# Grouped attention heads: maxima in pairs on the halves of the rows, keys two tiles at a time, sums and one row copy moved between engines

## The chip, the cores and the metric

The kernel runs on one core of a Trainium2 chip. The metric is device time in microseconds (us) of one execution. Engines: PE is TensorE (PEld its weight loads), DVE is VectorE, ACT is ScalarE, POOL is GpSimd, SP is SyncE, which issues DMAs here. Each engine runs its own instructions in the order written and waits on semaphores for the others.

## What is computed

One layer of a diffusion backbone over 256 context tokens and 2048 latent tokens: a mixing sublayer (differential attention, grouped-query attention and a Mamba-2 scan, side by side), an output projection, and a SwiGLU FFN. The change is in the grouped-query attention of the latent tokens: four query heads of width 64, two key heads, 2048 latent and 512 cached keys:

```
s = jnp.einsum('bqkgd,bskd->bkgqs', qb, k) * 64 ** -0.5
p = jax.nn.softmax(s, axis=-1)
o = jnp.einsum('bkgqs,bskd->bqkgd', p, v)
```

## The kernel before, in words

The work is cut into eight *units* of one key head j and 512 query tokens, both query heads of that key head (r = 0, 1) together. A unit needs two things in turn.

`maxima` (L945) finds, for each query row, the largest score over the 2560 keys. For each r and each block q of 128 queries TensorE multiplies the 128 stacked rows of the queries (64 rows of the value rounded to fp32r and 64 rows of the remainder, tile qa) with the keys (`gk[j][:, 0]`, which holds the same 64 rows twice), 512 keys at a time, into a bank of PSUM (tile gm, L959). VectorE reduces each bank to one column (gmx, L960). There are 40 such pieces, in two banks that alternate (tag "t"). Then the maxima are reduced to one negated value (nm, L962), eight transposes turn them into rows (gpt, L967), and VectorE copies each row to row 64 of tile qb (L968), so that the score matmul itself subtracts the maximum.

`weighted` (L971) walks over 20 tiles of 128 keys. For a tile: four score matmuls into one of two double banks (gs, L981 over 128 rows, L982 over 65), one exp on ScalarE (ge, L984), and, two tiles later, the product with the values into half the columns for each r (gpo, L990), and the addition of the exps to a running sum, on VectorE for eight of the 20 tiles, on GpSimd for twelve (L998, L1000). The first tile of each engine is only kept, so VectorE adds seven times and GpSimd eleven. Five exp tiles are in flight. A short tail (`unit_tail`, L1006) adds the two sums (L1009), turns the result (gpx), sums over keys by 16 small matmuls (gpl, L1020) and divides, during the next unit.

The order is written out by hand: `weighted` is a generator with two stops for each key tile, and the loop at L1339 to L1347 advances the maxima of the *next* unit by one piece at each stop, and at every second stop the tail, the context attention (`contexts`, in units 1 to 3) and the split of the output weights (`weights`, L1392, from unit 4 on: load w_out by 128 rows, ScalarE rounds it, VectorE subtracts, L1399). SP's DMAs alone are placed by the framework's scheduler in this part. Maxima of unit 0 run ahead, in the last steps of the differential heads, on 1024 keys at a time in the double banks (`wide`); unit 7 has none to run for a next one.

Buffers that matter: banks "t", two of 512 columns, also used by transposes; banks "s", two of 1024 columns; ge 5 tiles; wor 2 tiles.

Of the kernel before, what the change touches and what calls it, by code (L numbers as in the profile page):

```python
# [21 lines left out]
KEYS = LAT + PAST  # L22
NKT = KEYS // 128
# [13 lines left out]
def run(gen):  # L37
    for _ in gen:
        pass
# [802 lines left out]
def attention(tc, I, rx, op, ada_group, const, cst, ident, identr, stk_d, v_d, mix_d, rstd_from, row_bc):  # L842
    nc = tc.nc
    V, S, G, PE = nc.vector, nc.scalar, nc.gpsimd, nc.tensor
    i2 = cst[:, C_I2:C_I2 + 64]
    dscale, gscale = 32 ** -0.5, 64 ** -0.5

    with ExitStack() as ax:
        kv = ax.enter_context(tc.tile_pool(name="kv", bufs=2, reuse_waits="tile"))
        ps_s = ax.enter_context(tc.tile_pool(name="aps_s", bufs=2, space=PSUM, reuse_waits="tile"))  # L850
        ps_t = ax.enter_context(tc.tile_pool(name="aps_t", bufs=2, space=PSUM, reuse_waits="tile"))

        def load(out, src, q=nc.sync):

            q.dma_start(out=out.bitcast(F32), in_=src)
# [78 lines left out]
        gp, gk, gv, gqs, nms = {}, [], [], {}, []  # L934

        def group_queries(ui):
            j, u = units[ui]
            t0 = CTX + 512 * u
            qa, qb = [kv.tile([128, 2, 512], F32R, name=f"q{a}{ui}", tag="q") if ui % 2 else
                      gp[0].tile([128, 2, 512], F32R, name=f"q{a}{ui}", tag=f"q{a}") for a in "ab"]  # L940
            load(qa, stk_d[8 + 2 * j:10 + 2 * j, :, t0:t0 + 512].rearrange("r p t -> p r t"))
            load(qb[0:64], stk_d[8 + 2 * j:10 + 2 * j, 0:64, t0:t0 + 512].rearrange("r p t -> p r t"))
            gqs[ui] = qa, qb

        def maxima(ui, wide=False):  # L945
            j, u = units[ui]
            qa, qb = gqs[ui]
            nm = nms[ui % 2]
            mx = c1.tile([128, 8, 5], F32, name=f"gmx{ui}", tag="gmx", bufs=2)
            for r in range(2):  # L950
                for q in range(4):
                    ql = qa[:, r, 128 * q:128 * q + 128]
                    pieces = range(0, KEYS, 1024 if wide else 512)
                    for i, c in enumerate(pieces):
                        w = min(KEYS - c, pieces.step)
                        ps = (ps_s if wide else ps_t).tile([128, pieces.step], F32, name=f"gm{ui}_{r}{q}{c}",
                                                           tag="s" if wide else "t")
                        for e in range(0, w, 512):
                            PE.matmul(ps[:, e:e + 512], ql, gk[j][:, 0, c + e:c + e + 512], start=True, stop=True)  # L959
                        V.tensor_reduce(mx[:, 4 * r + q, i:i + 1], ps[:, 0:w], AX.X, ALU.max)  # L960
                        yield
            V.tensor_reduce(nm[:, :, 64], mx[:, :, 0:len(pieces)], AX.X, ALU.max, negate=True)  # L962
            yield
            for r in range(2):
                pt = ps_t.tile([128, 4, 128], F32R, name=f"gpt{ui}_{r}", tag="t")
                for q in range(4):
                    PE.transpose(pt[0:66, q], nm[:, 4 * r + q], identr)  # L967
                V.tensor_copy(qb[64:65, r], pt[64:65].rearrange("p q t -> p (q t)"))  # L968
                yield

        def weighted(ui, sp, ps_o, tails):  # L971
            j, u = units[ui]
            qa, qb = gqs.pop(ui)
            po = ps_o.tile([128, 512], F32, name=f"gpo{ui}", tag="o")
            acc, held, es = {}, {}, {}
            for kt in range(NKT + 2):
                if kt < NKT:
                    ks = slice(128 * kt, 128 * kt + 128)
                    ps = ps_s.tile([128, 1024], F32, name=f"gs{ui}_{kt}", tag="s").rearrange("p (r t) -> p r t", r=2)
                    for r in range(2):  # L980
                        PE.matmul(ps[:, r], gk[j][:, 0, ks], qa[:, r], start=True, stop=False)  # L981
                        PE.matmul(ps[:, r], gk[j][0:65, 1, ks], qb[0:65, r], start=False, stop=True)  # L982
                    e = es[kt] = sp.tile([128, 2, 512], F32, name=f"ge{ui}_{kt}", tag="ge", bufs=5)
                    S.activation(e, ps, AF.Exp, scale=gscale)  # L984
                yield
                if kt >= 2:
                    k = kt - 2
                    e = es.pop(k)
                    for r in range(2):
                        PE.matmul(po[64 * r:64 * r + 64, :], gv[j][:, k], e[:, r],  # L990
                                  start=(k == 0), stop=(k == NKT - 1))
                    eng, nm = (V, "v") if k % 5 in (1, 3) else (G, "g")
                    if nm not in acc:
                        if nm not in held:
                            held[nm] = e
                        else:
                            acc[nm] = sp.tile([128, 2, 512], F32, name=f"ga{nm}{ui}", tag=f"ga{nm}")
                            eng.tensor_tensor(acc[nm], held[nm], e, ALU.add)  # L998
                    else:
                        eng.tensor_tensor(acc[nm], acc[nm], e, ALU.add)  # L1000
# [128 lines left out]
        with ExitStack() as dx:  # L1129
            sp = dx.enter_context(tc.tile_pool(name="dsp", bufs=2, reuse_waits="tile"))  # L1130
            ps_o = dx.enter_context(tc.tile_pool(name="dps_o", bufs=1, space=PSUM, reuse_waits="tile"))
# [127 lines left out]
            side, tails = ada(), iter(())  # L1259
            pvs = []  # L1260
            for step in range(4 * n + 7):
# [15 lines left out]
                a, b, c, d, v = at(0), at(1), at(2), at(3), at(4)  # L1277
# [47 lines left out]
        gsp = ax.enter_context(tc.tile_pool(name="gsp", bufs=2, reuse_waits="tile"))  # L1325
        ps_o = ax.enter_context(tc.tile_pool(name="gps_o", bufs=1, space=PSUM, reuse_waits="tile"))
        cpool = ax.enter_context(ExitStack())
        csp = cpool.enter_context(tc.tile_pool(name="ctx", bufs=2, reuse_waits="tile"))
        ctx = contexts(csp, ps_o)
        tails = [normed(gsp, heads[3].o, heads[3].rl[:, :, 0], n, "l3", store_latents(3))]  # L1330
        for ui in range(len(units)):
            more = iter(())
            if ui + 1 < len(units):
                group_queries(ui + 1)
                more = maxima(ui + 1)
            if ui == 1:
                gv.append(group_values(1))
                gk.append(group_keys(1))
            for i, _ in enumerate(weighted(ui, gsp, ps_o, tails)):  # L1339
                next(more, None)  # L1340
                if i % 2:
                    if tails and next(tails[0], run) is run:
                        tails.pop(0)
                    if 1 <= ui < 4:
                        next(ctx, None)
                    if ui >= 4:
                        next(wo, None)  # L1347
# [37 lines left out]
class OutProj:  # L1385
# [6 lines left out]
    def weights(self, pool):  # L1392
        nc = self.tc.nc
        for k in range(8):
            raw = pool.tile([128, 1024], F32, name=f"wor{k}", tag="wor")
            nc.sync.dma_start(out=raw, in_=self.I["w_out"][128 * k:128 * k + 128, :])
            yield
# [749 lines left out]
```

## Time and profile before

| what | value |
|---|---|
| median of 3 runs | 3765.96 us (3758.62 to 3768.18) |
| profiled execution | 3772.03 us, span 3770.2 us |
| busy shares | PE 95%, DVE 66%, ACT 47%, POOL 48% |
| chain that ended last | PE 75%, DVE 9%, POOL 6% |
| granted TensorE clock, mean | 0.969 of full speed |

A busy share is the part of the span in which the engine ran an instruction. The chain is the work that ended last, followed back at each step to what released it. A row of the order of time gives start, duration, engine, line, operation, out<-in by tile names, shapes and count; consecutive instructions of a kind are merged. In brackets stands the idle time before, and what ended it. Matmul ends are modelled and overlap, so a matmul's price is read from start to start.

### The profile page before, as it was taken

The page shows a single profiled execution, that of the slowest core. Times are in us where ns is not written, and L with a number is a line of the kernel's source. Part 1 is how long each engine was busy: PE and PEld are TensorE (multiplying, and loading weights), DVE is VectorE, ACT ScalarE, POOL GpSimd, SP SyncE. Part 2 cuts the span into 40 slices and gives each one's busy share as a digit, 9 for nine tenths or more (in the row PEclk, how much of TensorE's full clock was granted, in tenths as well). Part 3 has the DMA queues.
Part 4 walks back from the last instruction along what each step waited for, and adds up shares of the span by engine and source line. Part 5 has one row for each costly group of instructions (what it writes and reads, how often), then busy time and mean ns, then how long its engine had stood idle before and what let it go on. Part 6 is the DMA issues. An engine that isn't in the chain of part 4 may idle for free.

```text
span 3770.2 us, 53905 instructions
## 1 busy us (share of the span) xinstructions
PE 3586.9 (95%) x20178; PEld 2884.0 (76%) x20178; DVE 2490.2 (66%) x4092; ACT 1787.6 (47%) x2890; POOL 1797.8 (48%) x1448
## 2 busy tenths in 40 slices
PE   6999899988999999999999989999999999999998
PEld 4888699984555555454458879999999999888886
DVE  3666766658889888767746776656556555465476
ACT  3555545546888885444334443334334333333232
POOL 3334356645788886445544567774233232011011
PEclk8999899998999999999999999999999999999999
DMA  5111244345311103001014656665454444645464
GB/s 199 49 46 46 76 126 124 119 130 164 97 34 42 36 22 83 14 26 48 23 62 165 209 190 216 213 216 182 153 186 164 160 154 163 231 160 175 153 217 156
DMA packets 265797, 473.65 MB, mean 126 GB/s; under 512 B 43480, under 2 KB 165752, under 8 KB 260928
## 3 DMA queue, kind: packets, MB, share of 16 engines
q1 hardware_dynamic: 247584, 456.72, 36.7%
q10 hardware_dynamic: 17232, 11.09, 1.1%
q8 instruction: 160, 2.62, 0.3%
q0 software_dynamic: 720, 2.38, 0.2%
q14 instruction: 101, 0.83, 0.1%
HBM read 345.72 MB, written 124.40 MB: 125 GB/s over the span
## 4 chain that ended last, share of the span: by engine, by line
PE 75%; DVE 9%; POOL 6%; issue 4%; DMA 3%; ACT 2%; SPq 0%; POOLq 0%; DVEq 0%; ACTq 0%
PE f L1685 6%; PE f L1684 6%; PE f L1683 6%; PE fy L1960 5%; PE fy L1962 5%; PE fy L1961 5%; PE ps L1174 4%; PE po L1234 4%; PE gpo L990 4%; PE px L225 3%; PE pt L1223 3%; PE gm L959 3%; PE gs L981 2%; PE gs L982 2%; PE opo L1447 2%
## 5 line engine op out<-in xcount | busy, mean ns | idle before, releaser
L1179 DVE TENSOR_SCALAR_CACHE_REDUCE e<-ps 128x1024 f32<-128x1024 f32 (+1 forms) x384 | 392.9, 1040 | 68.5 <-PE ps L1174 67.2
L1190 ACT ACTIVATE e<-e,nb 128x2560 f32<-128x2560 f32 x128 | 311.0, 2430 | 41.0 <-DVE nb L1184 40.9
L1960 PE MATMUL fy<-fp 128*128 128x512 f32 x792 | 308.7, 390 | 0.6 <-DVE fu L1823 0.6
L1962 PE MATMUL fy<-fp 128*128 128x512 f32 x792 | 308.7, 390 | 0.0
L1961 PE MATMUL fy<-fp 128*128 128x512 f32 x792 | 308.4, 389 | 0.0
L1212 POOL TENSOR_TENSOR e<-e,e 128x512 f32<-128x512 f32 x254 | 296.5, 1167 | 21.2
L1924 DVE TENSOR_TENSOR fp<-fo,fp 128x1536 fp32r<-128x1536 f32 (+1 forms) x110 | 208.7, 1911 | 140.5 <-ACT fp L1923 118.0
L960 DVE TENSOR_REDUCE gmx<-gm 128x1 f32<-128x512 f32 (+1 forms) x304 | 214.2, 715 | 120.0 <-PE gm L959 116.8
L1823 POOL TENSOR_TENSOR ft<-fu,fa 128x384 f32<-128x384 f32 x66 | 104.2, 1578 | 390.8 <-DVE fu L1823 342.8
L1991 POOL TENSOR_TENSOR fr<-fr,ln2b 128x1024 f32<-128x1024 f32 x17 | 54.0, 3178 | 490.6 <-DMA fo<-h_d 294.6
L1174 PE MATMUL ps<-dk,dq 96*128 96x512 f32 x640 | 244.9, 466 | 29.8 <-DVE e L1179 18.1
L1000 POOL TENSOR_TENSOR gag<-gag,ge 128x1024 f32<-128x1024 f32 x80 | 208.4, 2605 | 125.7 <-ACT ge L984 124.4
L984 ACT ACTIVATE ge<-gs 128x1024 f32<-128x1024 f32 x160 | 163.7, 1024 | 217.7 <-PE gs L982 215.3
L1923 ACT ACTIVATE fp<-fo 128x1536 fp32r<-128x1536 f32 (+1 forms) x110 | 157.2, 1442 | 195.1 <-PE fy L1962 163.8
L1211 POOL TENSOR_SCALAR e<-e,c 128x512 f32<-128x512 f32 x254 | 180.7, 711 | 115.2 <-DVE c L1203 104.9
L1174 PEld LDWEIGHTS ps<-dk,dq 96*128 96x128 f32 x640 | 101.0, 198 | 156.8 <-issue 72.1
L1224 ACT ACTIVATE wT<-pt 128x512 f32<-128x512 f32 x320 | 178.7, 591 | 67.8 <-PE pt L1223 67.1
L1234 PE MATMUL po<-wT,vl 128*64 128x256 f32 x1280 | 204.5, 407 | 0.0
L1223 PEld LDWEIGHTS pt<-cst,e 128*128 128x128 f32 x1280 | 160.7, 142 | 56.5 <-POOL e L1212 12.5
L1223 PE MATMUL pt<-cst,e 128*128 128x128 f32 x1280 | 197.1, 276 | 4.8 <-POOL e L1212 3.2
L225 PE MATMUL px<-xhTrue,wx 128*128 128x260 f32 (+2 forms) x864 | 182.1, 303 | 16.5 <-DVE l L374 7.0
L1685 PE MATMUL f<-fxt,wc 128*128 128x384 f32 x528 | 179.1, 339 | 2.6 <-DVE wc L1791 2.6
(454 smaller groups left out, 10613.0 us busy)
## 6 DMA issues: line engine op xcount, KB each, us to landing
fo<-in_wfo SPq DMA_DIRECT2D x110, 512.0 KB, 4.2
wq<-in_wfi SPq DMA_DIRECT2D x88, 512.0 KB, 3.7
wq<-ws_d SPq DMA_DIRECT2D x88, 512.0 KB, 4.2
h_d<-h SPq DMA_DIRECT2D x66, 384.0 KB, 3.0
wada<-in_w_ada SPq DMA_DIRECT2D x24, 1024.0 KB, 6.9
ws_d<-wq SPq DMA_DIRECT2D x44, 512.0 KB, 2.6
fo<-h_d SPq DMA_DIRECT2D x66, 256.0 KB, 4.1
fr<-x2T_d SPq DMA_DIRECT2D x20, 768.0 KB, 7.6
```

Source lines behind the costliest of these rows:

```text
L225: PE.matmul(out, l, r, start=(i == 0), stop=(i == n - 1))
L1174: PE.matmul(ps[:, 512 * c:512 * c + 512], Q[0:96, m, qs], K[0:96, m, k0:k0 + 512], start=True, stop=True)
L1179: V.tensor_scalar(self.e[m][:, k0:k0 + w], ps[:, c:c + w], dscale, -3.4e38, ALU.mult, ALU.max, accum_out=mx[:, m, seen[m]:seen[m] + 1])
L1190: S.activation(self.e[m], self.e[m], AF.Exp, bias=self.nb[:, m:m + 1], accum_out=self.l[:, m:m + 1])
L1212: G.tensor_tensor(e0[:, a:b], e0[:, a:b], e1[:, a:b], ALU.add)
L1223: PE.transpose(pt[:, k], self.e[0][:, 128 * (4 * g + k):128 * (4 * g + k) + 128], ident)
L1234: PE.matmul(po[64 * e:64 * e + 64], hd.v[:, k + e], self.wT[:, k + e], start=(k == 0), stop=(k == NKT - 2))
L1683: PE.matmul(o, w[:, 0, c, cs], x[:, 0, k], start=(k == 0), stop=False)
L1685: PE.matmul(o, w[:, 1, c, cs], x[:, 0, k], start=False, stop=(k == 3))
L1960: PE.matmul(o, x[:, 0, ts_], x[:, 0, hs], start=(f == 0), stop=False)
L1961: PE.matmul(o, x[:, 0, ts_], x[:, 1, hs], start=False, stop=False)
L1962: PE.matmul(o, x[:, 1, ts_], x[:, 0, hs], start=False, stop=(f == NF - 1))
```

## The change

- In `maxima` a piece is now a pair: for a block of queries and 512 keys, r = 0 on rows 0 to 63 and r = 1 on rows 64 to 127, of the rounded half of the queries alone (the remainder is left out of the maximum). Both read tile qb, whose lower half gets the rounded rows of r = 1 by a third load. Each matmul of a pair writes its own bank "t" (both in one double bank when wide). There are 20 stops of two matmuls instead of 40 of one; the wide form has 20 pieces instead of 24. The two transposed rows follow without a stop; the copy for r = 1 is on ScalarE.
- `weighted` takes two key tiles per round: eight score matmuls, a stop, then the value matmuls and additions of two tiles, a stop. The first round issues the matmuls that don't need the maxima first. VectorE gets five of the 20 tiles (k % 4 == 1), so four additions; GpSimd fifteen, so fourteen. Six exp tiles are in flight.
- The loop advances maxima, tail, context and weights once at each stop (21 stops a unit instead of 44).
- The output weights are loaded into one buffer, shared with a tile of another name, and used five stops later instead of two.

```
-            load qa, qb[0:64]
+            load qa, qb[0:64]; load(qb[64:128, 0], stk_d[9 + 2 * j, 0:64, t0:t0 + 512])
 maxima:
-            for r in range(2):
-                for q in range(4):
-                    for i, c in enumerate(pieces):
-                        PE.matmul(ps[:, e:e + 512], ql, gk[j][:, 0, c + e:c + e + 512], start=True, stop=True)
-                        V.tensor_reduce(mx[:, 4 * r + q, i:i + 1], ps[:, 0:w], AX.X, ALU.max)
-                        yield
+            for q in range(4):
+                for i in range(5):
+                    ...
+                    for r in range(2):
+                        hs = slice(64 * r, 64 * r + 64)
+                        PE.matmul(ps[r], qb[hs, 0, 128 * q:128 * q + 128], gk[j][hs, 0, 512 * i:512 * i + 512],
+                                  start=True, stop=True)
+                    if wide:
+                        V.tensor_reduce(mx[:, q::4, i], p, AX.X, ALU.max)
+                    else:
+                        for r in range(2):
+                            V.tensor_reduce(mx[:, 4 * r + q, i:i + 1], ps[r], AX.X, ALU.max)
+                    yield
 ...
-                V.tensor_copy(qb[64:65, r], pt[64:65].rearrange("p q t -> p (q t)"))
-                yield
+                if r: S.activation(qb[64:65, r], row, AF.Copy)
+                else: V.tensor_copy(qb[64:65, r], row)
 weighted:
+            def scores(kts):      # all first matmuls (128 rows), then per tile the second ones and the exp
+            def values(k):
+                ... value matmuls of tile k ...
+                eng, nm = (V, "v") if k % 4 == 1 else (G, "g")      # was k % 5 in (1, 3)
+            for kt in range(0, NKT + 2, 2):
+                if kt == 0:
+                    scores((0, 1))
+                elif kt < NKT:
+                    scores((kt,))
+                    scores((kt + 1,))
+                yield
+                if kt >= 2:
+                    values(kt - 2)
+                    values(kt - 1)
+                    yield
 loop:
-            for i, _ in enumerate(weighted(ui, gsp, ps_o, tails)):
+            for _ in weighted(ui, gsp, ps_o, tails):
                 next(more, None)
-                if i % 2: tail, ctx, wo
+                tail, ctx, wo
 weights:
-            raw = pool.tile([128, 1024], F32, name=f"wor{k}", tag="wor")
+            raw = pool.tile([128, 1024], F32, name=f"wor{k}", tag="osq", bufs=1)
             nc.sync.dma_start(out=raw, in_=self.I["w_out"][128 * k:128 * k + 128, :])
-            yield
+            for _ in range(4):
+                yield
```

## Rows read from the trace of the kernel before

**Rows 1.** Busy us of each engine (instructions) by unit, PEclk, DMA share, GB/s.

```profile
1535.60:1612.30 76.70, 69.94 (x294) 36.68 (x292) 56.20 (x105) 34.34 (x66) 30.73 (x14) 0.93 0.05 14
1612.30:1678.90 66.60, 66.60 (x295) 35.00 (x293) 41.36 (x77) 30.73 (x52) 32.52 (x16) 1.00 0.07 22
...
1736.20:1798.70 62.50, 57.90 (x231) 28.19 (x229) 53.04 (x61) 29.14 (x30) 30.61 (x12) 0.97 0.21 68
...
1854.90:1911.00 56.10, 55.42 (x231) 27.83 (x229) 39.09 (x53) 21.68 (x22) 29.65 (x12) 1.00 0.02 5
1911.00:1957.00 46.00, 44.90 (x182) 19.82 (x180) 14.10 (x12) 21.74 (x23) 27.41 (x12) 1.00 0.09 29
```

**Rows 2.** Chain that ended last, units 0 to 7: shares by line.

```profile
by line: PE gpo L990 28.2%; PE gm L959 18.0%; PE gs L981 14.9%; PE gs L982 14.6%; DVE gav L1000 4.1%; DVE gmx L960 3.9%; PE gpl L1020 2.5%; DVE wol L1399 2.0%; DVE gav L998 1.5%; issue 1.3%; PE poc L1107 1.0%; DVE qb L968 0.9%; PE pxc L1115
```

**Rows 3.** TensorE in time, unit 6: start, us, line, operation, shapes, count.

```profile
1897.41 0.50 PE L959 MATMUL gm<-gk,qa 128*128 128x512 f32 x1
1897.75 0.39 PE L981 MATMUL gs<-qa,gk 128*128 128x512 f32 x1
...
1898.67 0.40 PE L959 MATMUL gm<-gk,qa 128*128 128x512 f32 x1
1899.01 1.08 PE L990 MATMUL gpo<-ge,vg 128*64 128x512 f32 x4
1900.01 0.50 PE L959 MATMUL gm<-gk,qa 128*128 128x512 f32 x1
```

**Rows 4.** TensorE, unit 7, which has no maxima.

```profile
1946.48 0.50 PE L981 MATMUL gs<-qa,gk 128*128 128x512 f32 x1
...
1948.61 0.50 PE L981 MATMUL gs<-qa,gk 128*128 128x512 f32 x1
...
1954.00 2.79 PE L990 MATMUL gpo<-ge,vg 128*64 128x512 f32 x12
```

**Rows 5.** TensorE, context scores, 128 and 64 rows in turn (eight such).

```profile
1631.23 0.38 PE L1070 MATMUL psc<-ckq,cqa 128*128 128x256 f32 x1
1631.54 0.38 PE L1071 MATMUL psc<-ckq,cqa 64*128 64x256 f32 x1
```

**Rows 6.** TensorE, the scan's matmuls on the two halves of the rows.

```profile
316.69 0.70 PE L483 MATMUL po<-Sf,CT 64*128 64x256 f32 x4
317.32 0.39 PE L225 MATMUL px<-xhTrue,wx 128*128 128x260 f32 x1
```

**Rows 7.** VectorE in order of time, end of unit 6.

```profile
1904.92 1.25 DVE L1000 TENSOR_TENSOR gav<-gav,ge 128x1024 f32<-128x1024 f32 x1
...
1908.35 0.69 DVE L960 TENSOR_REDUCE gmx<-gm 128x1 f32<-128x512 f32 x1 [0.75 <-PE gm L959]
...
1909.19 2.15 DVE L1000 TENSOR_TENSOR gav<-gav,ge 128x1024 f32<-128x1024 f32 x1
```

**Rows 8.** GpSimd, the same stretch.

```profile
1902.70 2.38 POOL L1000 TENSOR_TENSOR gag<-gag,ge 128x1024 f32<-128x1024 f32 x1 [2.09 <-ACT ge L984]
1907.90 2.36 POOL L1000 TENSOR_TENSOR gag<-gag,ge 128x1024 f32<-128x1024 f32 x1 [2.82 <-ACT ge L984]
```

**Rows 9.** TensorE, from unit 6 to unit 7.

```profile
1907.81 0.50 PE L959 MATMUL gm<-gk,qa 128*128 128x512 f32 x1
...
1910.95 0.50 PE L981 MATMUL gs<-qa,gk 128*128 128x512 f32 x1
1912.12 0.50 PE L982 MATMUL gs<-qb,gk 65*128 65x512 f32 x1 [0.67 <-DVE qb L968]
```

**Rows 10.** VectorE groups, 1481 to 1960: busy us, mean ns | idle before.

```profile
L1000 DVE TENSOR_TENSOR gav<-gav,ge 128x1024 f32<-128x1024 f32 x48 | 72.8, 1516 | 22.2 <-ACT ge L984 22.2
...
L1399 DVE TENSOR_TENSOR wol<-wor,woh 128x1024 fp32r<-128x1024 f32 x8 | 14.6, 1824 | 0.0
```

**Rows 11.** Loads of the output weights (tile wor).

```profile
DMA to landing us min/median/max: 3.2/3.3/6.8
```

**Rows 12.** VectorE, the sum that closes unit 7.

```profile
1957.72 1.23 DVE L1009 TENSOR_TENSOR gav<-gav,gag 128x1024 f32<-128x1024 f32 x1 [3.18 <-POOL gag L1000]
```

More of the change, by code (lines that the diff above doesn't have):

```diff
@@ L942, in group_queries @@
             load(qb[0:64], stk_d[8 + 2 * j:10 + 2 * j, 0:64, t0:t0 + 512].rearrange("r p t -> p r t"))
+            load(qb[64:128, 0], stk_d[9 + 2 * j, 0:64, t0:t0 + 512])
             gqs[ui] = qa, qb
@@ L946, in maxima @@
             j, u = units[ui]
-            qa, qb = gqs[ui]
+            qb = gqs[ui][1]
             nm = nms[ui % 2]
             mx = c1.tile([128, 8, 5], F32, name=f"gmx{ui}", tag="gmx", bufs=2)
-            for r in range(2):
-                for q in range(4):
-                    ql = qa[:, r, 128 * q:128 * q + 128]
-                    pieces = range(0, KEYS, 1024 if wide else 512)
-                    for i, c in enumerate(pieces):
[L955 to L958, printed above, removed]
-                            PE.matmul(ps[:, e:e + 512], ql, gk[j][:, 0, c + e:c + e + 512], start=True, stop=True)
-                        V.tensor_reduce(mx[:, 4 * r + q, i:i + 1], ps[:, 0:w], AX.X, ALU.max)
-                        yield
-            V.tensor_reduce(nm[:, :, 64], mx[:, :, 0:len(pieces)], AX.X, ALU.max, negate=True)
+            for q in range(4):
+                for i in range(5):
+                    nm_ = f"gm{ui}_{q}{i}"
+                    if wide:
+                        p = ps_s.tile([128, 1024], F32, name=nm_, tag="s").rearrange("p (r t) -> p r t", r=2)
+                        ps = [p[:, r] for r in range(2)]
+                    else:
+                        ps = [ps_t.tile([128, 512], F32, name=f"{nm_}{r}", tag="t") for r in range(2)]
+                    for r in range(2):
+                        hs = slice(64 * r, 64 * r + 64)
+                        PE.matmul(ps[r], qb[hs, 0, 128 * q:128 * q + 128], gk[j][hs, 0, 512 * i:512 * i + 512],
+                                  start=True, stop=True)
+                    if wide:
+                        V.tensor_reduce(mx[:, q::4, i], p, AX.X, ALU.max)
+                    else:
+                        for r in range(2):
+                            V.tensor_reduce(mx[:, 4 * r + q, i:i + 1], ps[r], AX.X, ALU.max)
+                    yield
+            V.tensor_reduce(nm[:, :, 64], mx, AX.X, ALU.max, negate=True)
             yield
@@ L967, in maxima @@
                     PE.transpose(pt[0:66, q], nm[:, 4 * r + q], identr)
-                V.tensor_copy(qb[64:65, r], pt[64:65].rearrange("p q t -> p (q t)"))
-                yield
+                row = pt[64:65].rearrange("p q t -> p (q t)")
+                if r:
+                    S.activation(qb[64:65, r], row, AF.Copy)
+                else:
+                    V.tensor_copy(qb[64:65, r], row)
         def weighted(ui, sp, ps_o, tails):
@@ L975, in weighted @@
             acc, held, es = {}, {}, {}
[L976 to L979, printed above, removed]
+            def scores(kts):
+                ps = [ps_s.tile([128, 1024], F32, name=f"gs{ui}_{kt}", tag="s").rearrange("p (r t) -> p r t", r=2)
+                      for kt in kts]
+                for kt, p in zip(kts, ps):
@@ L980, in weighted @@
                     for r in range(2):
[L981 to L984, printed above, removed]
+                        PE.matmul(p[:, r], gk[j][:, 0, 128 * kt:128 * kt + 128], qa[:, r], start=True, stop=False)
@@ new lines, in scores @@
+                for kt, p in zip(kts, ps):
+                    for r in range(2):
+                        PE.matmul(p[:, r], gk[j][0:65, 1, 128 * kt:128 * kt + 128], qb[0:65, r],
+                                  start=False, stop=True)
+                    e = es[kt] = sp.tile([128, 2, 512], F32, name=f"ge{ui}_{kt}", tag="ge", bufs=6)
+                    S.activation(e, p, AF.Exp, scale=gscale)
+            def values(k):
+                e = es.pop(k)
+                for r in range(2):
+                    PE.matmul(po[64 * r:64 * r + 64, :], gv[j][:, k], e[:, r], start=(k == 0), stop=(k == NKT - 1))
+                eng, nm = (V, "v") if k % 4 == 1 else (G, "g")
+                if nm not in acc:
+                    if nm not in held:
+                        held[nm] = e
+                    else:
+                        acc[nm] = sp.tile([128, 2, 512], F32, name=f"ga{nm}{ui}", tag=f"ga{nm}")
+                        eng.tensor_tensor(acc[nm], held[nm], e, ALU.add)
+                else:
+                    eng.tensor_tensor(acc[nm], acc[nm], e, ALU.add)
@@ L985, in weighted @@
+            for kt in range(0, NKT + 2, 2):
[4 more added lines that the diff above has]
+                    scores((kt + 1,))
                 yield
                 if kt >= 2:
[L987 to L1000, printed above, removed]
@@ L1338, in attention @@
                 gk.append(group_keys(1))
-            for i, _ in enumerate(weighted(ui, gsp, ps_o, tails)):
+            for _ in weighted(ui, gsp, ps_o, tails):
                 next(more, None)
[L1341 to L1347, printed above, removed]
+                if tails and next(tails[0], run) is run:
+                    tails.pop(0)
+                if 1 <= ui < 4:
+                    next(ctx, None)
+                if ui >= 4:
+                    next(wo, None)
             run(more)
```

1 line of the change is left out of this document (removed).

## The prediction

> **What bounds the kernel now.** I read the page first, then the stretch of the grouped heads unit by unit, then its chain of waits, then single steps of TensorE, VectorE and GpSimd. The change touches only this stretch (about 1444 to 1957 us of 3770.2). It is eight units (0 to 7) of 20 key tiles. [rows 1] has five of them: units 1, 2, 4, 6 and 7. Unit 6 is a plain one: 56.1 us, TensorE busy 55.42 of them, VectorE 39.09, ScalarE 21.68, GpSimd 29.65. Units 1 and 2 also carry the context attention (76.7 and 66.6 us), unit 4 the split of the output weights (62.5), and unit 7 has no maxima for a next unit (46.0). The chain [rows 2] lies on the matmuls gpo, gm and gs for 28.2 + 18.0 + 14.9 + 14.6 = 76% of the stretch: TensorE sets the pace, and the maxima (gm) are the part of it that can shrink. VectorE has 17 us of slack in a plain unit, but only because its two banks for gm decouple it from TensorE.
>
> **The steady step on TensorE.** One key tile takes 2.60 us (gm at 1897.41 to gm at 1900.01) [rows 3]. The first matmul after a gpo takes 0.34 until the next, then each takes 0.23 (1897.75 to 1898.67 is four); the last one before gpo again 0.34; gpo 1.00. So two tiles cost 5.20. A tile more of gpo in the same run costs 0.85: twelve matmuls, three tiles, take 2.79 with entry and tail [rows 4].
>
> After the change two tiles are: eight gs, a pair, two gpo, a pair. Does a pair run side by side? No maxima do so now, but the scan's matmuls on the two halves of the rows do: four of 64 rows by 256 columns, fp32, are done in 0.63 (316.69 to 317.32) [rows 6]. One such fp32 pass of 512 columns on the full depth costs 0.43 (2.79 for six double steps) [rows 4], so of 256 it costs 0.21, four in a row 0.85, two side by side 0.43 plus entry and exit. I take it that the pair runs side by side. Its bare price is then 0.23. Each change of the array's shape costs more: matmuls of 128 and of 64 rows in turn, 256 columns each, follow at 0.31 [rows 5], where half of 0.23 would be 0.12; so 0.2 for a change, of which 0.1 falls before and 0.1 after it. The bounds for a pair with its changes are 0.23 (changes free) and 0.63 (two whole changes); I take 0.43, the value of [rows 5] with each change shared with its neighbour.
>
> The Trainium skill, "TensorEngine Tiling (Array Packing)", section Tiling Modes (Key Properties), says that a change of the tiling mode drains TensorE. That speaks against the change, as each pair stands between two other shapes; [rows 5] agrees with it. By that rule the pairs would eat their own gain wherever they stand between full-depth matmuls; here gpo, which uses half the columns, changes the shape anyway.
>
> New two-tile step: gs 0.34 + 7 x 0.233 + 0.1 = 2.07; pair 0.43; gpo 1.01 + 0.85 = 1.86; pair 0.43; sum 4.80 against 5.20. That is -0.2 a tile, -4.0 a unit, **-28.0** for the seven units with maxima. In unit 7 the step falls from 2.13 (1946.48 to 1948.61 [rows 4]) to (2.07 + 1.86) / 2 = 1.965: -3.4.
>
> **What takes it back: VectorE behind both banks.** Today a gm waits for the reduction before the last one. A pair takes both banks, so it waits for both reductions of the pair just before. Count from a pair's start: its first reduction starts 0.54 later (1907.81 on TensorE [rows 9], 1908.35 on VectorE [rows 7]), two take 1.4, so the banks are free at 1.95, and TensorE asks for them at 2.3 (over gpo) or 2.5 (over gs). That fits, with 0.35 to 0.55 to spare. Now put in an addition (one in two double steps, k = 5, 9, 13, 17). Queued behind it on VectorE are the next pair's reductions, and behind these TensorE. Alone it takes 1.25: it ends at 3.2, the next reductions at 4.6, the next pair but one is wanted at 4.8: no loss. But it waits for GpSimd: the add at 1909.19 took 2.15 and ended 1.08 after the GpSimd add of 1907.90 ended; the one at 1904.92, where GpSimd had 0.16 left, took 1.25 [rows 7, 8]. GpSimd gets 14 additions a unit for 11, three of 2.37 in a round of four tiles (9.6 us), so it runs 74% of the time, with 1.2 left on average when it does. Then the add holds VectorE for 2.4, to 4.4, the reductions end at 5.8, and the pair wanted at 4.8 starts its second half at 5.8: 1.0 lost. Bounds: 0 (GpSimd idle) and 2.2 (a whole GpSimd addition ahead). I take 1.0, four a unit, seven units: **+28.0**. Today's adds take 1516 ns on average [rows 10], 0.27 over the free one, with GpSimd busy 53% of unit 6 [rows 1] instead of 74%.
>
> The Trainium skill, "SBUF — State Buffer", section SBUF: two separate sides, calls this an exclusive lock that whoever starts first holds for the whole instruction. The two adds agree. By that rule the loss can't pass one GpSimd instruction for each add, which is my upper bound.
>
> **Unit ends.** The last two pairs follow each other with nothing between: the second is wanted after 0.43 and gets its banks at 2.0: +1.55. The row copies, one on ScalarE now, come while gpo of two tiles and the four first score matmuls run, so the present stall is gone: gs at 1912.12 came 1.17 after the one before instead of 0.34 [rows 9]: -0.85. The third tile of scores then waits for the first exp: +0.2. Net +0.9 x 7 = **+6.3**. The sixth exp buffer and one more load of 64 rows per unit cost nothing: by the steps above TensorE first reads the loaded tile some 9 us after the last scores release its place, and SP's queue holds nothing then but these loads and the unit's store; were it late, each microsecond would count for each unit.
>
> **The weight split** (8 times) now goes through one buffer, five steps apart (some 12 us), while such a load needs 3.3 (6.8 at most) [rows 11]: hidden; were SP held up, ScalarE and VectorE would wait for it in order. Its subtraction takes 1.82 on average with GpSimd's interference [rows 10], and costs 62.5 - 56.1 = 6.4 today, 0.8 each. With VectorE's slack down to some 0.35, 1.5 each: **+5.6**. Bounds -6.4 (hidden) and +8.2.
>
> **Context units.** They cost 76.7 + 66.6 - 2 x 56.1 = 31.1 over plain ones. Over unit 6 TensorE is busier by 14.5 + 11.2 = 25.7, VectorE by 17.1 + 2.3 = 19.4 [rows 1]: 45.1 in series, so 14.0 is covered today. Without the second bank I let half the cover go: **+7.0**, bounds 0 and +14.0.
>
> **Unit 7's end.** Its last two tiles are both GpSimd's now, and the sum that closes the unit waits for the later one, as it does today at 1957.72 [rows 12]. After the last exp that is one addition of 2.36 and the rest of another, some 1.4 more; with the -3.4: **-2.0**. The chain to the output projection starts there, so all of it counts.
>
> **Unit 0's maxima** (wide, before 1481): 40 x 0.233 + 24 x 0.1 = 11.7 becomes 20 x 0.53 = 10.7 (a pair between full-depth shapes): **-1.0**; the reductions keep their columns.
>
> Sum: -28.0 + 28.0 + 6.3 + 5.6 + 7.0 - 2.0 - 1.0 = +15.9. The profiled execution took 3772.0 (span 3770.2), 6 above the median of 3766.0, so I forecast 3766 + 16 = 3782, +0.4%. Its own range, with adds between 0.75 and 1.25 (+-7) and context between 3 and 11, is 3771 to 3793.
>
> **Rivals.**
> 1. *GpSimd is out of the way when the adds come* (faster). The adds cost nothing: +15.9 - 28.0 = -12, 3754. Place: the four adds of a unit; the point: GpSimd must have less than about 0.2 left when the first pair's reductions end. For it: the add at 1904.92 met just that [rows 7, 8]. Against: GpSimd is then 74% busy.
> 2. *Half of it* (no change). The adds cost 0.5, and the context units stay: +15.9 - 14.0 - 7.0 = -5, 3761. For it: adds and exps are both tied to TensorE's steps, so a round may settle at a good phase; against: the wait of [rows 7].
> 3. *The pair runs one after the other*, so that the change doesn't do what it says. TensorE then needs 140 x 0.23 = 33 more, part of it under VectorE's lateness; a third of it in view gives +11: 3793. Against it [rows 6]; for it: no pair of this type in the trace.
>
> **Chances.** The measurement can't tell less than 0.3% (11.3 us) from no change. Forecast 0.52, rival 1 0.18, rival 2 0.20, rival 3 0.10. Slower: 0.75 of the forecast and all of rival 3, 0.49. Same: the rest of the forecast and nine tenths of rival 2, 0.31. Faster: rival 1 and the rest of rival 2, 0.20. The range 3757 to 3797 leaves out most of rival 1 and the far ends of the unknown costs.
>
> **What would show it.** In the changed trace: two gm within 0.1 of each other (pair side by side; 0.23 apart: rival 3); steps of 4.8 for two tiles where no add falls, and about 1 longer where one does, with gav at 2 and more and the following gm waiting for gmx; unit 6 at about 57; units 1 and 2 together at 150; unit 7 at 44. A plain unit of 53 would prove rival 1, and wide waits of DVE for wor would break the weight term.

## The result, and the profile after

The changed kernel takes **3788.82 us** (median; 3777.45 to 3789.91), the kernel before 3764.02 on the same chip: ratio 1.0059 [1.0041, 1.0076], 24.8 us slower. The forecast was slower, by 15.9. The profiled execution after took 3789.13 (span 3787.3), 17.1 over that of before. The grouped heads account for +31.0 of these; the stretch ahead of them was 11.6 shorter and the one behind 2.2, in code that is the same. The 11.6 go with TensorE's granted clock: ahead of unit 0 the kernel before spent 174.1 us at half clock in this execution and the changed one 150.2, and half of the difference is 12. One execution of e4_before_no_pool below took 6804.28, and that kernel's median is over its other three.

Units again run from the first score matmul of one to that of the next. Unit 7 goes in these rows to just before the sum that closes it, as in [rows 1], and in the table further down to its last division. Busy time by engine for units 1, 2, 4, 5, 6 and 7, the view of [rows 1]:

```profile
1523.20:1612.70 89.50, 73.44 (x295) 37.65 (x294) 55.56 (x99) 34.43 (x68) 38.00 (x16) 0.83 0.05 14
1612.70:1686.30 73.60, 68.65 (x297) 35.02 (x294) 42.86 (x75) 30.62 (x54) 42.01 (x20) 0.93 0.07 20
...
1744.40:1811.10 66.70, 60.14 (x231) 28.60 (x229) 45.23 (x53) 25.15 (x28) 41.13 (x15) 0.88 0.16 49
1811.10:1875.90 64.80, 58.98 (x231) 28.29 (x229) 45.77 (x53) 25.08 (x27) 40.36 (x15) 0.90 0.14 44
1875.90:1931.70 55.80, 53.16 (x230) 26.66 (x229) 37.22 (x48) 21.05 (x23) 38.65 (x15) 0.99 0.02 6
1931.70:1976.00 44.30, 42.00 (x188) 21.95 (x185) 9.23 (x7) 22.12 (x25) 36.90 (x15) 1.00 0.10 30
```

The plain unit 6 did not grow (56.1 before); units 1 and 2 grew by 12.8 and 7.0, unit 4 by 4.2, and unit 5, plain before, by 8.6. Where a unit grew, the granted clock (third figure from the end) fell too: 0.83 and 0.93 in units 1 and 2, against 0.93 and 1.00, and 0.88 in unit 4, against 0.97.

TensorE in unit 6, the view of [rows 3]. A round has two pairs (`gm` x2): one follows the values (gpo), the other the scores (gs). From a pair that follows the values to the next such pair is a step of two tiles. The first row gives the first and the last start of the pair at 1890.65:

```profile
L963 PE MATMUL gm<-gk,qb x2: 500/500/500, 1890.7 to 1890.7; 64*128 64x512 f32 x2
1890.65 0.50 PE L963 MATMUL gm<-gk,qb 64*128 64x512 f32 x2
1891.08 0.74 PE L995 MATMUL gs<-qa,gk 128*128 128x512 f32 x2
...
1893.14 0.50 PE L963 MATMUL gm<-gk,qb 64*128 64x512 f32 x2
1893.58 1.94 PE L1006 MATMUL gpo<-ge,vg 128*64 128x512 f32 x8
1895.45 0.50 PE L963 MATMUL gm<-gk,qb 64*128 64x512 f32 x2
...
1897.94 0.98 PE L963 MATMUL gm<-gk,qb 64*128 64x512 f32 x2
...
1900.72 0.50 PE L963 MATMUL gm<-gk,qb 64*128 64x512 f32 x2
...
1905.51 0.50 PE L963 MATMUL gm<-gk,qb 64*128 64x512 f32 x2
...
1908.56 1.09 PE L963 MATMUL gm<-gk,qb 64*128 64x512 f32 x2 [0.48 <-DVE gmx L969]
...
1911.44 0.50 PE L963 MATMUL gm<-gk,qb 64*128 64x512 f32 x2
```

The two matmuls of a pair start together (less than 0.1 apart, the sign that the prediction asked for), take 0.50 together, and the next work starts 0.43 after the pair: they run side by side. A step without an addition takes 4.80 (1890.65 to 1895.45). Those with one take 5.27 (1895.45 to 1900.72) and 5.93 (1905.51 to 1911.44), and in each a pair comes late: the pairs at 1897.94 and 1908.56 take 0.98 and 1.09 instead of 0.50, the second matmul waiting for its bank, and the pair at 1908.56 waited 0.48 for the first bank as well. VectorE, then GpSimd, in the same stretch:

```profile
1894.88 2.29 DVE L1013 TENSOR_TENSOR gav<-ge,ge 128x1024 f32<-128x1024 f32 x1
1897.10 2.67 DVE L969 TENSOR_REDUCE gmx<-gm 128x1 f32<-128x512 f32 x4
...
1904.95 2.94 DVE L1015 TENSOR_TENSOR gav<-gav,ge 128x1024 f32<-128x1024 f32 x1
1907.83 2.56 DVE L969 TENSOR_REDUCE gmx<-gm 128x1 f32<-128x512 f32 x4
```
```profile
1893.72 18.84 POOL L1015 TENSOR_TENSOR gag<-gag,ge 128x1024 f32<-128x1024 f32 x7
```

GpSimd adds without a gap for 18.84 us, the two VectorE additions take 2.29 and 2.94 instead of 1.25, and four reductions then run without a gap: VectorE is behind by a pair, and TensorE waits for it. Groups of VectorE, units 0 to 6, the view of [rows 10]:

```profile
L1015 DVE TENSOR_TENSOR gav<-gav,ge 128x1024 f32<-128x1024 f32 x21 | 49.8, 2372 | 0.0
L1013 DVE TENSOR_TENSOR gav<-ge,ge 128x1024 f32<-128x1024 f32 x7 | 15.4, 2193 | 0.0
L1425 DVE TENSOR_TENSOR wol<-wor,woh 128x1024 fp32r<-128x1024 f32 x8 | 15.2, 1903 | 1.0 <-ACT woh L1424 1.0
```

The chain of waits of the changed execution does not lead back through the units, so nothing answers [rows 2]. TensorE's own waits in the grouped heads (us in total, times, longest) stand in for it; first before, then after:

```profile
PE gm L959 <- DVE gmx L960: 11.0, 11, 2.1
PE gs L982 <- DVE qb L968: 3.6, 6, 0.7
```
```profile
PE gm L963 <- DVE gmx L969: 27.1, 17, 6.1
PE ptc L1124 <- DVE gmx L969: 6.2, 8, 0.8
PE gs L995 <- ACT ge L1001: 5.0, 10, 1.2
PE pxc L1141 <- DVE gmx L969: 1.2, 6, 0.2
```

The wait for the row copies is gone, as forecast. New are the waits of ptc and pxc: these matmuls of the context attention use the same two banks "t" as the pairs. That GpSimd holds the exp tiles too long is hardly the cause: in the changed execution ScalarE's exps waited once for a GpSimd addition, for 1.2.

### The profile page after: what moved, and what is told of

It is laid out like the page before. It is cut to its first block, busy times and chain, and to the rows that moved or that the text cites. A ratio compares the mean times of both kernels' runs of the same rounds, so it can differ in the third digit from the quotient of the medians.

```text
span 3787.3 us, 53927 instructions
## 1 busy us (share of the span) xinstructions
PE 3577.3 (94%) x20178; PEld 2873.9 (76%) x20178; DVE 2469.7 (65%) x4056; ACT 1784.6 (47%) x2898; POOL 1872.8 (49%) x1472
## 5 line engine op out<-in xcount | busy, mean ns | idle before, releaser
L1205 DVE TENSOR_SCALAR_CACHE_REDUCE e<-ps 128x1024 f32<-128x1024 f32 (+1 forms) x384 | 392.7, 1039 | 67.4 <-PE ps L1200 66.4
L1216 ACT ACTIVATE e<-e,nb 128x2560 f32<-128x2560 f32 x128 | 311.0, 2430 | 41.0 <-DVE nb L1210 40.9
L1015 POOL TENSOR_TENSOR gag<-gag,ge 128x1024 f32<-128x1024 f32 x104 | 280.9, 2701 | 75.6 <-ACT ge L1001 69.4
L969 DVE TENSOR_REDUCE gmx<-gm 128x1 f32<-128x512 f32 x280 | 180.0, 684 | 142.5 <-PE gm L963 142.1
```

Source lines behind the costliest of these rows:

```text
L1205: V.tensor_scalar(self.e[m][:, k0:k0 + w], ps[:, c:c + w], dscale, -3.4e38, ALU.mult, ALU.max, accum_out=mx[:, m, seen[m]:seen[m] + 1])
L1216: S.activation(self.e[m], self.e[m], AF.Exp, bias=self.nb[:, m:m + 1], accum_out=self.l[:, m:m + 1])
```

## The experiments

The theory tested is the forecast's: VectorE's additions wait for GpSimd, and since a pair needs both banks, TensorE waits behind them. The rival is that another part of the change costs, GpSimd's three additions more or the order of two tiles. All kernels were timed beside the kernel before. The table has each kernel's profile by kind of unit (us, worked out from the starts of the units; "half" is the time at half clock in all eight). These columns come from one profiled execution each. "Change" is the median against that of before on the same chip:

| run | 0+3+6 plain | 1+2 context | 4+5 weights | 7 | half | change |
|---|---|---|---|---|---|---|
| before | 167.6 | 143.2 | 118.7 | 51.9 | 19.3 | |
| after | 169.3 | 163.1 | 131.4 | 50.4 | 84.4 | +24.8 |
| e1_split_before | 173.1 | 166.7 | 129.5 | 47.4 | 83.0 | +30.9 |
| e2_split_alone | 167.5 | 143.5 | 116.3 | 52.4 | 25.3 | -5.7 |
| e3_after_no_pool | 155.5 | 145.9 | 110.6 | 47.4 | 23.9 | -25.7 |
| e4_before_no_pool | 164.7 | 133.0 | 110.4 | 50.6 | 0.8 | -27.5 |
| e5_after_all_pool | 165.8 | 155.9 | 114.4 | 56.1 | 67.4 | +2.6 |
| e6_before_all_pool | 164.3 | 148.2 | 113.8 | 55.7 | 29.1 | -4.2 |
| e7_pairs_alone | 180.7 | 151.7 | 129.0 | 56.0 | 81.6 | +25.7 |
| e8_filler | 169.0 | 168.4 | 135.2 | 51.1 | 38.3 | +35.2 |
| e9_two_tiles_single | 159.0 | 147.1 | 128.4 | 50.8 | 34.3 | +3.9 |
| e10_two_tiles_single_split | 158.5 | 150.3 | 121.6 | 52.6 | 41.9 | -3.4 |
| e11_after_no_wol | 171.3 | 163.8 | 111.2 | 51.3 | 66.0 | +3.7 |
| e12_mixed | 160.2 | 145.3 | 123.9 | 52.8 | 37.2 | -4.9 |

**The split of the additions, in both kernels** (e1_split_before: the changed kernel; e2_split_alone: the kernel before).

```
e1:  - eng, nm = (V, "v") if k % 4 == 1 else (G, "g")
     + eng, nm = (V, "v") if k % 5 in (1, 3) else (G, "g")
e2:  the reverse
```

e1 

> The changed kernel with the additions divided as before (eight key tiles of 20 on VectorE, so seven additions, eleven on GpSimd). My theory (VectorE is late behind both banks, each addition of its own costs a wait for GpSimd and then a stall of TensorE): three more additions of 1.25 us a unit on VectorE outweigh the three fewer of 2.37 on GpSimd, as every one of them stands before a pair; plain units (0, 3, 6) about 1.5 us longer each than in the changed kernel, the whole 0 to +8 us against it, so +25 to +33 against the kernel before. Rival A (fourteen GpSimd additions are what is too much, whatever VectorE does): plain units shorter by 2 or more, the whole 15 to 25 us faster than the changed kernel, close to the kernel before. Rival B (neither; the cost is in the context and weight units alone): plain units unchanged, the whole within 4 us of the changed kernel.

e2 

> The kernel before with only the new division of the additions (four on VectorE, fourteen on GpSimd a unit); maxima singly, one tile at a time. My theory: with a bank between, VectorE's lateness is hidden, so the new division alone costs little: plain units 55.5 to 56.5, the whole within 6 us of the kernel before (context units up to 3 us longer each). Rival A (fourteen GpSimd additions are too much as such): +10 to +20 us.

Measured: 3793.72, ratio 1.0078 [1.0056, 1.0100]; and 3757.15, ratio 0.9986 [0.9977, 0.9996]. With GpSimd back at eleven additions the changed kernel is no faster (+30.9 against +24.8), and with fourteen the kernel before is no slower, but a little faster. The fourteen additions by themselves are not the fault.

**GpSimd's additions left out, in both kernels** (only the first of a unit stays, so the sums are not complete; the closing sum adds 1.0, which the lines below leave out). That is 13 additions a unit fewer in e3 and ten in e4.

```
-                else:
+                elif eng is V:
                     eng.tensor_tensor(acc[nm], acc[nm], e, ALU.add)
```

e3 

> The changed kernel without GpSimd's additions but the first of each unit; the closing sum adds 1.0 so that no divisor is zero, so the output is not the reference's. My theory (two of VectorE's waits for GpSimd make each addition cost 1 us of TensorE, the same in context and weight units): plain units 52 to 53.5 instead of 55 to 58, units 1, 2, 4, 5 down by 12, 7, 11, 9 us, the stretch 35 to 50 us shorter than in the changed kernel. Rival B (the context and weight units suffer from the coarser steps, not from GpSimd): plain units as theory, but units 1, 2, 4, 5 together no more than 10 us shorter.

e4 

> Control: the kernel before without GpSimd's additions but the first of each unit, with the same 1.0 in the closing sum (output not the reference's). My theory: with a bank between, GpSimd's additions cost the plain units next to nothing (55 to 56.1), and only units 1 and 4, where VectorE is nearly full, gain some 7 us each: 12 to 25 us less than the kernel before, so some 20 us less gain than the same step brings in the changed kernel. Rival A (GpSimd's additions cost the same in both): the gain equals that of the changed kernel within 5 us.

Measured: 3737.17, ratio 0.9927 [0.9911, 0.9943], so 50.5 under the changed kernel (24.8 + 25.7, each against before on its chip); and 3735.31, ratio 0.9931 [0.9905, 0.9956], 27.5 under before. GpSimd's additions cost some 23 us more in the changed kernel, which is nearly its whole loss; without them the two kernels can't be told apart. The eight units of e3 are 54.7 shorter than those of the changed kernel, a little more than expected. Units 1 and 6 of e3, then TensorE's waits in units 0 to 7:

```profile
1518.40:1595.20 76.80, 68.62 (x295) 35.09 (x293) 43.44 (x99) 34.19 (x68) 3.69 (x3) 0.91 0.05 16
...
1827.40:1879.80 52.40, 51.28 (x232) 25.72 (x229) 32.89 (x49) 21.09 (x23) 3.47 (x2) 1.00 0.02 6
```
```profile
PE ptc L1124 <- DVE gmx L969: 5.7, 8, 0.8
PE gm L963 <- DVE gmx L969: 4.9, 8, 0.8
PE gs L995 <- ACT ge L1001: 4.6, 10, 1.2
```

The same units of e4:

```profile
1525.00:1591.40 66.40, 64.75 (x294) 34.20 (x292) 49.02 (x104) 34.20 (x66) 4.72 (x4) 1.00 0.06 17
...
1824.20:1879.30 55.10, 55.09 (x230) 27.87 (x228) 37.63 (x53) 21.66 (x22) 3.46 (x2) 1.00 0.02 6
```

The wait of `gm` falls from 27.1 to 4.9 and unit 6 to 52.4. What stays is ptc, and scores that wait for exps (4.6, of which 2.8 in units 1 and 2). Unit 1 is 10.4 longer than its counterpart even here, and both context units 12.9, at a granted 0.91 in unit 1 against 1.00. TensorE waits there for the banks "t" that the pairs hold, without GpSimd's help (ptc and pxc, 6.9), and for the banks "s", which exps and the context's own scores give back late (4.3); these are no matter of the pairs' two banks.

**All additions on GpSimd, in both kernels** (no closing sum).

```
-  eng, nm = (V, "v") if k % 4 == 1 else (G, "g")      # e6: k % 5 in (1, 3)
+  eng, nm = G, "g"
-  V.tensor_tensor(acc["v"], acc["v"], acc["g"], ALU.add)
```

e5 

> The changed kernel with all twenty additions of a unit in one sum on GpSimd, none on VectorE, and so no closing sum. My theory (VectorE's additions wait for GpSimd while TensorE needs both of its banks): with no addition in VectorE's queue the wait is gone, although GpSimd has five additions more (19 x 2.37 = 45 us in a unit of some 53); 28 to 45 us shorter than the changed kernel's 3789, at 3744 to 3761, plain units at 52 to 53. Rival (GpSimd is simply the bound, or its load on the memory is the fault): with 19 additions it is worse, 3789 or longer, plain units at 57 or more.

e6 

> The kernel before with all additions on GpSimd in the same way. Theory: single maxima have a bank in hand, so VectorE's waits cost little there; 5 to 15 us shorter than before (the split by four alone gave 5.7). If the gain is that of the same edit in the changed kernel (28 or more), the pairs have nothing to do with it.

Measured: 3766.95, 22.2 under the changed kernel; 3760.12, 4.2 under before. Both fell short of the gains expected (28 to 45, 5 to 15). Five additions more on GpSimd make the changed kernel faster, so it is the additions' place in VectorE's queue that costs, not GpSimd's load. Two units of e5 are longer than in the changed kernel: unit 7 (56.1 against 50.4), where TensorE waits at the end for the last of GpSimd's additions, and unit 6 (59.9 against 55.9). The first row is that wait in unit 7; then TensorE in unit 6, with the busy time of the first 17.2 us of the unit:

```profile
PE gpl L1044 <- POOL gag L1015: 7.5, 1, 7.5
1846.28 0.68 PE L976 MATMUL gpt<-identr,nm 128*66 128x128 f32 x8 [1.99 <-DVE nm L971]
...
1856.01 2.79 PE L1006 MATMUL gpo<-ge,vg 128*64 128x512 f32 x8
...
1873.22 0.50 PE L963 MATMUL gm<-gk,qb 64*128 64x512 f32 x2
...
1878.02 0.50 PE L963 MATMUL gm<-gk,qb 64*128 64x512 f32 x2
```
```profile
1846.80:1864.00 17.20, 17.20 (x61) 10.64 (x58) 4.51 (x7) 6.20 (x7) 7.28 (x4) 0.62 0.00 1
```

The later step is 4.80 again, without a wait; unit 6 is long because TensorE, after a wait of 1.99, did its first 17.2 us at a granted 0.62.

**Pairs alone** (one tile at a time, one pair in each, additions as before).

```
before + the paired `maxima` and the load of qb[64:128, 0]
-                next(more, None)
+                if i % 2 == 0 or i > 40:
+                    next(more, None)
```

> The kernel before with the maxima in pairs alone: one tile of keys at a time, a pair in each, the additions split as before, both row copies on VectorE. Theory: a tile's step is 1.14 + 0.43 + 1.01 = 2.58 on TensorE, as before, and the pair takes both banks, so an addition that waits costs up to 0.6; with seven additions in seven units 0 to 29 us longer than before, I take +12, plain units 57 to 59. Rival (it is the order of two tiles that costs, the pairs alone are harmless or a gain): -5 to +2.

Measured: 3789.97, ratio 1.0058 [1.0044, 1.0071]: +25.7, inside the range but twice the value taken. The pairs alone bring a loss as large as the whole; the order of two tiles is not needed for it. The loss falls in other units, though: the plain ones grew by 13.1 (54.0, 65.0 and 61.7, where 57 to 59 was expected) against 1.7 in the changed kernel, the context units by 8.4 against 19.9. TensorE, then VectorE:

```profile
1889.41 0.50 PE L963 MATMUL gm<-gk,qb 64*128 64x512 f32 x2
...
1891.97 0.50 PE L963 MATMUL gm<-gk,qb 64*128 64x512 f32 x2
...
1894.87 1.10 PE L963 MATMUL gm<-gk,qb 64*128 64x512 f32 x2 [0.27 <-DVE gmx L969]
```
```profile
1891.15 3.07 DVE L1008 TENSOR_TENSOR gav<-ge,ge 128x1024 f32<-128x1024 f32 x1
```

A tile takes 2.56 where nothing waits, as before (2.60). Behind an addition of 3.07 the next pair waits 0.27 for its first bank and takes 1.10 instead of 0.50.

**Filler for TensorE** (the changed kernel, units 1, 2, 4 and 5).

```
+ for p in ps:
+     for r in range(2):
+         PE.matmul(p[:, r], gk[j][:, 0, 0:128], qa[:, r], start=True, stop=True)
```

> The changed kernel with two matmuls more ahead of the scores of each tile in units 1, 2, 4 and 5 (they write where the scores then start afresh, and are read by nobody): 160 matmuls of 0.23, 37 us of TensorE. Theory (TensorE's stalls lower its granted clock, and the half clock is some 17 us of the surplus): TensorE idles less, the time at half clock in these four units falls from 70 us to under 25, and the units get longer by less than half of the added work, or shorter: -15 to +15 us. Rival (the clock falls for another reason, and the surplus is all VectorE's waiting): half-clock time stays near 70, and the units get longer by 15 to 37.

Measured: 3799.55, 10.4 over the changed kernel. Units 1 and 5:

```profile
1523.90:1613.90 90.00, 75.70 (x335) 42.14 (x334) 55.12 (x99) 34.87 (x67) 36.61 (x16) 0.94 0.05 14
...
1815.50:1884.40 68.90, 64.36 (x271) 34.03 (x270) 41.54 (x53) 25.97 (x27) 39.62 (x15) 0.95 0.16 48
```

In the four units the time at half clock fell from 70.3 to 23.9, and 37 us of added work cost 9.1. So the clock rose when TensorE was given more to do, and the rival is out. The traces also say where the 28 saved come from. TensorE's busy time in the four units rose from 261.2 to 276.8, by 15.6 for 37 of added work, so the same work took some 21 less at the higher clock; its idle time fell from 33.4 to 26.8, by 7 that the filler merely fills.

**Two tiles without pairs** (e9: single maxima, four in the scores of two tiles, weights through one buffer as in the change; e10: also the new split and one row copy on ScalarE).

```
+ for r in range(2):
+     PE.matmul(ps[:, r], gk[j][:, 0, ks], qa[:, r], start=True, stop=False)
+     PE.matmul(ps[:, r], gk[j][0:65, 1, ks], qb[0:65, r], start=False, stop=True)
+     if r: ... exp
+     yield
+ ... after two tiles: values(kt - 2); values(kt - 1)
```

e9 

> The kernel before with the order of two tiles alone: eight score matmuls with one single full-depth maximum after every second of them, then four value matmuls in one run; additions split as before, weights through one buffer as in the change. Theory (the pairs that take both banks are the fault, the longer run of value matmuls is a gain): a step of two tiles is 12 x 0.233 + 0.34 + 0.1 + 1.6 = 4.85 on TensorE against 5.20, up to -3.5 a unit where VectorE follows; four maxima in some 3 us need 2.8 of VectorE, so additions cost part of it; -25 to -5 us on the whole, I take -12. Rival (the order of two tiles is at fault as well): 0 to +15.

e10 

> The kernel before with all of the change but the pairs: two tiles with single maxima as in the run beside it, four additions of a unit on VectorE (the split that alone gave -5.7), one row copy on ScalarE. Theory: the gains add up, -30 to -8 us against before, I take -17, which would beat both kernels. Rival: VectorE's additions wait longer behind a busier GpSimd and the split no longer gains; equal to the run beside it or longer.

Measured: 3768.16, ratio 1.0004 [0.9993, 1.0014]; 3760.94, ratio 0.9990 [0.9981, 0.9999]. Both missed. The plain units did gain (159.0 and 158.5 against 167.6), but the context and weight units gave it back (in e9 +3.9 and +9.7). There the waits of `gm` for VectorE came to 22.0 in e9, against 9.6 before: four maxima in a row within three microseconds leave VectorE little room, as pairs do. In the weight units no run splits this from the weights' one buffer.

**The changed kernel without the weights' subtraction.**

```
- nc.vector.tensor_tensor(self.wl[:, k], raw, self.wh[:, k], ALU.subtract)
+ nc.scalar.activation(self.wl[:, k], raw, AF.Copy)
```

> The changed kernel with the weights' subtraction left out (the low half of the output weights becomes a plain copy on ScalarE, so this part of the computation is changed). Theory: the subtraction waits for GpSimd as the additions do, and units 4 and 5 (66.7 and 64.7 us) fall to about 56 to 58 each, the whole by 10 to 18 us to 3771 to 3779. Rival (units 4 and 5 are long for the additions and the clock alone): they stay above 61, the whole falls by less than 7.

Measured: 3768.02, 21.1 under the changed kernel, a little more than expected. Units 4 and 5:

```profile
1744.00:1799.90 55.90, 53.21 (x231) 26.74 (x229) 37.33 (x49) 28.71 (x31) 38.67 (x15) 0.99 0.19 59
1799.90:1855.20 55.30, 52.64 (x232) 26.24 (x229) 37.36 (x49) 28.84 (x32) 38.59 (x15) 1.00 0.17 51
```

Eight subtractions cost the changed kernel 2.6 each, with the clock, which is lower where they stand (0.88 and 0.90 against 0.99 and 1.00).

**A mixed version** (e10, with the order of two tiles in units 0, 3, 6 and 7 only).

```
- for kt in range(NKT + 2):
+ for kt in range(NKT + 2 if ui in (1, 2, 4, 5) else 0):   # else two tiles, as in e10
```

> A version put together from the runs: single maxima everywhere, the order of two tiles only in units 0, 3, 6 and 7 (52.3, 53.1, 53.1, 52.4 in the run with that order and the new split), one tile at a time in units 1, 2, 4 and 5 (76.9, 66.6, 59.3, 57.0 in the run of the split alone), four additions on VectorE, one row copy on ScalarE, weights through one buffer. Theory (the longer run of value matmuls gains where VectorE has nothing else to do, and costs where it has): the units add up to 470.7 against 481.4 before, so 8 to 14 us shorter than before, about 3753, and 3 to 8 us shorter than the split alone. Rival (a unit is long or short by its phase against GpSimd and by the granted clock, not by its order): the sum comes back to about 480, no more than 5 us from before.

Measured: 3759.12, ratio 0.9993 [0.9983, 1.0002]: the rival was right. Units 0, 3, 6 and 7 kept their times within 2 us, but units 4 and 5 came to 123.9 instead of 116.3, with the weights through one buffer over two units. The lowest median of all versions that compute the whole result is that of the new split alone (3757.15, 5.7 under before), but this one and e6 (4.9 and 4.2 under) are too near to tell apart from it.

## Why the prediction was right in direction and short in size

**Right.** *The pair* runs side by side at 0.43 (forecast 0.43), so rival 3 is out. *The step* of two tiles is 4.80 to the hundredth. *What takes it back* is VectorE behind both banks: unit 6 shows it, and e3 and e5 (each against the same edit in the kernel before) and e7 support it from three sides. Without GpSimd's additions the plain units are 9.2 shorter than before's (e3 against e4), 3.1 each, and the forecast's -4.0 + 0.9 is -3.1. Rival 1 needed GpSimd out of the way, and the additions took 2.2 to 2.4 on average, as forecast. Rival 2 fell by its other half, context units that stay as they were; its price of an addition was the nearer one, as the next lines show. Two slips in the sum cancel: 20 x 0.53 is 10.6 and not 10.7, 20 x 0.165 is 3.3 and not 3.4.

**The added wait**, forecast at 1.0 per addition: three steps of unit 6 cost 0.47, 1.13 and 0.30 (the third 5.10, 1916.24 to 1921.34), so 0.63 on average, less than forecast. The *unit end* costs more: among other things the exps at a unit's start hold TensorE for 0.71 (before the scores of 1934.54) instead of 0.2. Together the plain units came to +0.6 each against +0.9, which is luck in part: by these three steps the additions would cost 2.5 a unit and not 4.0 (an estimate), and the unit ends made up for it. *Unit 7* came to -1.5 against -2.0, *unit 0's maxima* to -1.8 against -1.0. The loads through one buffer were hidden: VectorE waited 1.0 in all for the rounding that follows them.

**Too small: the context units.** Forecast +7.0 beside the plain +1.8, bounds 0 and +14.0; measured +19.9 in all, so 18.1 for this term. I had let half of the cover go. Without GpSimd's additions all of it is there already: these units are 12.9 longer (e3 against e4) where plain ones are 3.1 shorter each, 19.1 in all. The pairs hold both banks, and the context's transposes queue for the same two (ptc, 5.7 us), which I had not counted. Neither half of the change does it alone: in these units the pairs by themselves cost 8.4 (e7), two tiles with single maxima 3.9 (e9). My upper bound was TensorE and VectorE in series, with 25.7 of TensorE; it was passed since TensorE's busy time over that of unit 6 came to 35.8, in units with 40.9 us at half clock, against 10.2 before.

**Too small: the weights.** Forecast +5.6 beside +1.8; measured +12.7 for units 4 and 5, so 10.9, beyond the bound of 8.2. Without GpSimd's additions the two units are equal in both kernels (110.6 and 110.4), where plain ones get 3.1 shorter each: so 6.4 of the term is there without them, and 4.5 come with GpSimd. By e11 a subtraction costs 2.6, where I had 1.5. The pairs are not needed for this term either: with single maxima, but the weights through one buffer and over two units, units 4 and 5 took 128.4 (e9) and 123.9 (e12), against 118.7 before and 116.3 in e2; with pairs and the weights as before, 129.0 (e7). What the one buffer and its later place cost by themselves was not run. One place where pairs and weights meet, at the end of unit 5, TensorE, VectorE and GpSimd:

```profile
1854.23 0.63 PE L998 MATMUL gs<-qb,gk 65*128 65x512 f32 x2
1857.83 1.39 PE L963 MATMUL gm<-gk,qb 64*128 64x512 f32 x2 [2.98 <-DVE gmx L969]
1859.15 3.68 PE L1006 MATMUL gpo<-ge,vg 128*64 128x512 f32 x8
```
```profile
1852.14 1.72 DVE L1425 TENSOR_TENSOR wol<-wor,woh 128x1024 fp32r<-128x1024 f32 x1 [0.34 <-ACT woh L1424]
1853.78 3.40 DVE L1015 TENSOR_TENSOR gav<-gav,ge 128x1024 f32<-128x1024 f32 x1
1857.10 1.27 DVE L969 TENSOR_REDUCE gmx<-gm 128x1 f32<-128x512 f32 x2
```
```profile
1852.85 6.54 POOL L1015 TENSOR_TENSOR gag<-gag,ge 128x1024 f32<-128x1024 f32 x2
```
```profile
1856.65:1863.48 6.83, 5.65 (x12) 1.62 (x12) 3.02 (x5) 0.00 (x0) 2.74 (x1) 0.50 0.00 0
```

The last row has TensorE's granted clock, 0.50, from within the stall on. A subtraction and an addition stand in front of the reductions, the addition waits for GpSimd (3.40), TensorE stalls for 2.98, and the eight value matmuls behind the stall take 3.68 instead of 1.94. I had priced the two VectorE instructions each by itself, and a stall by its length only.

The steps that failed are these two terms: together 29.0 measured where the forecast had 12.6. Waiting and the clock weigh about the same. TensorE's idle time in the eight units rose from 16.9 to 46.5, by 29.6, and its busy time by only 3.2, though the forecast has its work 31 cheaper (28.0 and 3.4); the 65 us more at half clock can cost at most half of that, 32. What stays open is how much of the waiting was VectorE behind GpSimd and how much the coarser order of two tiles.

## What to carry to other kernels

Before one makes the bound engine's work cheaper by taking two buffers at once, count who else uses those buffers and what stands in the in-order queue of the engine that frees them: here 0.2 us gained in each tile was lost to additions that wait for another engine, and to context and weight work in the same queue. Price the rare instructions (context, weights) together with their neighbours in the queue, not one by one. And where the bound engine begins to idle in bits, look at its granted clock in that stretch: the stall can be paid again afterwards, at the lower clock.

## What the runs showed of the hardware

TensorE's granted clock fell from 2.4 to 1.2 GHz inside stretches where it was 82 to 93% busy (units 1, 2, 4 and 5 of the changed kernel): 19.3 us at the lower level in the eight units before, 84.4 after. It fell at 1847.53 in e5, behind a wait of 1.99 that ended at 1846.28, and at 1856.65 in the changed kernel, within a wait of 2.98. In e5 it stayed low for most of the next 17.2 us, while TensorE was busy without a gap (mean 0.62). With added work that nobody reads the granted clock was higher (e8, units 1 and 5: 0.94 and 0.95 instead of 0.83 and 0.90). Eight value matmuls took 3.68 at the lower level and 1.94 at the upper.

Two fp32r matmuls on the two halves of the rows, 512 columns each, start together and cost TensorE 0.43 between full-depth and half-column matmuls; one full-depth matmul of that length costs 0.23 in a run of its kind. VectorE's addition of two tiles of 128x1024 took 1.23 with GpSimd done [rows 12] and 2.94 and 3.40 beside GpSimd's additions.
